# Weight halves split one by one in the attention, kept in memory and reloaded slot by slot

## The chip, the cores and the metric

The kernel runs on one core of a Trainium2 chip. The metric is the device time of one launch in microseconds, as the median of several runs of the kernel. Profiles come from one execution each.

## The reference

Two layers work on 2048 latent tokens and 256 context tokens, 1024 wide, in float32. Layer 0 mixes a gated short convolution with a state-space scan in both directions. Layer 1 is latent attention: 16 heads, queries and keys of 64 + 32 elements (the 32 rotated), values of 64, every latent token attending to all 2304 tokens, then

```python
out_l = (att_l.reshape(b_, n, MLA_MIX) * jax.nn.silu(g_l)) @ w_out   # 2048 x 1024 @ 1024 x 1024
h = h + (gate[:, None] * out_l)
```

where the gate g_l is a 2048 x 1024 product of the normalized input with a 1024 x 1024 part of the layer's input weight, and gate is a vector of the modulation. The change concerns the two 1024 x 1024 weights of these products (the gate's and w_out) while the attention runs.

## The kernel before, in words

A float32 product is made of three float32r matmuls (mm3, lines 119 to 121): each operand is split into a high half (rounded to float32r) and a low half (the rest); high x high, high x low and low x high are summed in PSUM.

The attention is the last stage. It is software-pipelined by hand: one loop over steps t (from line 2129 on), 64 items (a head and a block of 512 queries) of 9 steps each, 576 steps, and a short tail. A step takes 256 of the 2304 keys. In step t the loop writes out, in this order, the scores of step t (6 matmuls, `scores`), the product of probabilities and values of step t - 16 (18 matmuls, `pv`, L2011), the copy of the scores from PSUM (ScalarE, L1929) and their running maximum (VectorE, L1941) of step t - 1, the conversion to f16 of t - 14 (ScalarE L1985, every third on GpSimd L1983), the exponential of t - 13 (ScalarE, L1975), the subtraction of the maximum of t - 12 (VectorE, L1970) and the low f16 half of t - 15 (GpSimd, L1991). The order that is written is the order on each engine's queue. The score PSUM has two buffers. All DMAs are issued on SyncE's queue (SP), which works them off in the order written.

Beside this run the side products, a generator `side` that is called three times in each step from step 7 on (`side_step`). One product (one mm3 of 512 columns) takes three calls, that is one step. There are six sets: the gate's columns 0 to 511 and 512 to 1023 (16 jobs of 8 products each, `gate_job`), and four sets of the output product (`out_job`): tokens of the first or second half of the blocks, with k 0 to 3 or 4 to 7 of the 8 slices of 128 head columns (in the last set only 4 and 5; 6 and 7 follow in `tail`). A set uses 8 weight slots of 128 x 512, each as high and low half (`wfs(0, s)`, `wfs(1, s)`), held in SBUF tiles named t, v and u. The left operand of a job comes by DMA into a tile named at (1 MB for a gate job, 512 KB or 256 KB for an output job), fetched one job ahead.

`products` runs one set. It first splits the set's 8 slots, one in three calls, so one per step; no product is issued in that time. For a gate slot ScalarE makes the high half (L1728) and GpSimd the low half (L1734). For an output slot, whose weight is scaled, GpSimd first multiplies by the modulation gate (L1740), ScalarE scales and rounds (L1730), VectorE makes the low half (L1736). The raw weights come by DMA into four tiles named raw, four ahead. The first set's slots 0 to 3 were split before the attention. Both halves of the output weight are split twice, for the first and for the second half of the tokens. Before a job whose tile was not fetched ahead, `products` waits two steps (`idle(2)`); an output job also waits until `turner` has gated, transposed and stored the heads that it needs. `turner` starts on a group of heads at the step `ready` of its last head; for the third output set that is step 442 of the schedule's count, and its first tile is stored some steps later.

`later(n, phase, fn)` writes out fn n steps on, at a named place in the step. `f_room` lets a new accumulation start only if one of the two PSUM tiles named fps is free.

Of the kernel before, what the change touches and what calls it, by code (L numbers as in the profile page):

```python
# [10 lines left out]
F32 = mybir.dt.float32  # L11
F32R = mybir.dt.float32r
# [45 lines left out]
def hybrid_conv_s5_mla_kernel(tc, x, c, ctx, c_ctx, mod_w, mod_b, norm_w, e_w_in, e_conv_w, e_lam_re, e_lam_im,  # L58
# [11 lines left out]
    with ExitStack() as top:  # L70
# [3 lines left out]
        def dt(name, shape, dtype=F32):  # L74
            return dr.tile(shape, dtype, name=name)
# [18 lines left out]
        gd = dt("gd", [16, P, D])  # L94
        ad = dt("ad", [16, P, D])
        atd = dt("atd", [16, P, 2, KD, P])

        def plain(a):
            return a.bitcast(F32) if a.dtype == F32R else a
# [1552 lines left out]
        with ExitStack() as at_:  # L1652
# [43 lines left out]
            def wfs(a, s):  # L1696
                return wf_tile(a, s)
# [22 lines left out]

            raw = []

            def w_split():
                w, s, n, scaled = raw.pop(0)

                def hi():
                    if scaled is None:
                        S.copy(out=wfs(0, s), in_=w)  # L1728
                    else:
                        S.activation(out=wfs(0, s), in_=w, func=AF.Copy, scale=invc[:, scaled:scaled + 1])  # L1730

                def lo():
                    if scaled is None:
                        GP.tensor_tensor(out=wfs(1, s), in0=w, in1=wfs(0, s).bitcast(F32), op=ALU.subtract)  # L1734
                    else:
                        V.scalar_tensor_tensor(out=wfs(1, s), in0=w, scalar=invc[:, scaled:scaled + 1],  # L1736
                                               in1=wfs(0, s).bitcast(F32), op0=ALU.mult, op1=ALU.subtract)

                if scaled is not None:
                    GP.tensor_tensor(out=w, in0=w, in1=g1[:, n], op=ALU.mult)  # L1740
                later(1, "pre", hi)
                later(1, "post", lo)
# [2 lines left out]
                for _ in range(3 * n):  # L1745
                    yield

            def products(slots, jobs, ahead, first=0):

                for x_ in range(first, len(slots)):  # L1750
                    yield
                    yield
                    w_split()
                    if x_ + 4 < len(slots):
                        w_raw(slots[x_ + 4:x_ + 5])
                    yield
                tiles = {}

                def fetch(m):
                    if m < len(jobs):  # L1760
                        tiles[m] = jobs[m][0]()

                for m, (_, mats, evac, need) in enumerate(jobs):
                    if m not in tiles:
                        while need and need not in turned:
                            yield from idle(1)
                        fetch(m)
                        yield from idle(2)
                    a, rest = tiles.pop(m)
                    for x_, (k, s) in enumerate(mats):  # L1770
                        yield
                        while x_ == 0 and not f_room():
                            yield
                        if x_ == 0:
                            ps = f_get()
                        mm3(ps, a[:, 0, k, :], a[:, 1, k, :], wfs(0, s), wfs(1, s), x_ == 0, x_ == len(mats) - 1)
                        yield
                        if m + 1 < len(jobs) and m + 1 not in tiles and not unstored and (
                                not jobs[m + 1][3] or jobs[m + 1][3] in turned):
                            fetch(m + 1)  # L1780
                        if x_ == len(mats) - 1:
                            evac(ps, rest)
                            if m == len(jobs) - 2:
                                w_raw(ahead[:4])
                        yield

            def gate_job(lt, n):
# [18 lines left out]
            def out_job(lt, n, k0, k1):  # L1806
                ns = slice(n * 512, (n + 1) * 512)
                j, b = lt // 2, lt % 2

                def load():  # L1810
                    a = big.tile([P, 2, KD, P], F32R, name="at", bufs=2)
                    ht = (wt.tile([P, 512], F32, name="raw", bufs=4) if k1 == 6 else wk.tile([P, 512], F32, name="fo"))
                    dma(out=a[:, :, k0:k1], in_=atd[lt, :, :, k0:k1])
                    dma(out=ht, in_=hd[lt, :, ns])
                    return a, ht

                def evac(ps, ht):
                    def add():
                        V.tensor_tensor(out=ht, in0=ps, in1=ht, op=ALU.add)
                        f_put()  # L1820

                    def store():
                        dma(out=(ol[b, :, j, ns] if k1 == KD else hd[lt, :, ns]), in_=ht)
                        unstored.discard((lt, n))

                    if k1 != 6:
                        unstored.add((lt, n))
                    later(1, "mid", add)
                    later(1, "post", store)

                return load, [(k, k % 4 + 4 * n) for k in range(k0, k1)], evac, (lt, k0)
# [5 lines left out]
            def turner():  # L1837

                for l0_, l1_, k0, k1, every in ((0, 8, 0, 4, 12), (0, 8, 4, 8, 6), (8, 16, 0, 4, 7), (8, 16, 4, 6, 4),
                                                (8, 12, 6, 7, 3), (12, 16, 6, 7, 3)):  # L1840
                    kn = k1 - k0
                    cs = slice(k0 * P, k1 * P)
                    for lt in range(l0_, l1_):
                        while now[0] < max(ready[lt // 4, k] for k in range(k0, k1)) or (now[0] + 5) % NP < 2:
                            yield
                        a = wk.tile([P, 512], F32, name="ta", bufs=3)
                        gt = wk.tile([P, 512], F32, name="tg", bufs=2)
                        dma(out=a[:, :kn * P], in_=ad[lt, :, cs])
                        dma(out=gt[:, :kn * P], in_=gd[lt, :, cs])

                        def gated(a=a, gt=gt, kn=kn):
                            GP.tensor_tensor(out=a[:, :kn * P], in0=a[:, :kn * P], in1=gt[:, :kn * P], op=ALU.mult)

                        later(3, "post", gated)

                        def turn(a=a, lt=lt, k0=k0, kn=kn):
                            ps = f_get()
                            for k in range(kn):
                                PE.transpose(ps[:, k * P:(k + 1) * P], a[:, k * P:(k + 1) * P], idf)
                            m = wk.tile([P, 2, 4, P], F32R, name="tm", bufs=1)  # L1860
                            pv = ps[:, :kn * P].rearrange("p (k n) -> p k n", k=kn)

                            def store():
                                dma(out=atd[lt, :, :, k0:k0 + kn], in_=m[:, :, :kn])
                                turned.add((lt, k0))

                            def low():
                                V.tensor_tensor(out=m[:, 1, :kn], in0=pv, in1=m[:, 0, :kn].bitcast(F32), op=ALU.subtract)
                                f_put()

                            later(1, "pre", lambda: S.copy(out=m[:, 0, :kn], in_=pv))
                            later(1, "mid", low)
                            later(1, "post", store)

                        later(5, "turn", turn)
                        turns_due.add(now[0] + 5)
                        for _ in range(every):
                            yield
# [11 lines left out]
                return [out_job(lt, n, k0, k1) for lt in range(l0_, l1_) for n in range(2)]  # L1890

            def side():
                yield from products(gslots(0), [gate_job(lt, 0) for lt in range(16)], gslots(1), first=4)
                yield from products(gslots(1), [gate_job(lt, 1) for lt in range(16)], kslots(0))
                yield from products(kslots(0), out_jobs(0, 8, 0, 4), kslots(4))
                yield from products(kslots(4), out_jobs(0, 8, 4, 8), kslots(0))
                yield from products(kslots(0), out_jobs(8, 16, 0, 4), kslots(4))
                yield from products(kslots(4), out_jobs(8, 16, 4, 6), [])


            vt_ = {}
# [204 lines left out]
            tails = [tail(2, total, total + 4, 0), tail(3, total + DP + 1, total + DP + 2, total + 8)]  # L2106
            sd = side()
            alive = [True]

            tn = turner()  # L2110

            def side_step():
                if alive[0] and next(sd, "end") == "end":
                    alive[0] = False

# [6 lines left out]
            while t < total + DP + 2 or alive[0] or agenda or tails:  # L2122
# [14 lines left out]
                if t > 6:  # L2137
                    side_step()
                next(tn, None)
                if t < total:  # L2140
                    g, h, qb = its[i]
                    if p == 0 and i + 1 < NI:
# [88 lines left out]
```

## Time and profile before

| what | us |
|---|---|
| median of 3 runs (3537.05 to 3541.81) | 3540.95 |
| the profiled execution | 3544.93 |
| its span | 3542.9 |
| TensorE busy in the span | 3241.8 |
| VectorE busy | 2633.4 |
| ScalarE busy | 2187.5 |
| GpSimd busy | 2153.3 |

The span runs from the first to the last instruction of the profiled execution. Matmuls are pipelined, and one begins before the one ahead of it has ended, so the distance of their starts is what one costs. An instruction's duration on VectorE can hold time in which it stands still. The granted clock of TensorE is given as a share of full speed; 1.00 is 2.4 GHz, 0.50 is 1.2 GHz. Copies of the scores (L1929) are counted to know how many steps a stretch holds.

### The profile page before, as it was taken

What the parts mean: (1) busy time and instruction counts of PE and PEld (TensorE: products, weight loads), DVE (VectorE), ACT (ScalarE), POOL (GpSimd) and SP (SyncE); (2) the same over time, 40 slices, a digit from 0 to 9 for tenths busy, and PEclk for the clock granted to TensorE, in tenths of its full rate; (3) what the DMA queues carried; (4) which work ended last, traced back from release to release, by engine and by line L of the source; (5) the groups of instructions that cost most, each with busy time, mean ns of one, the idle gap of its engine ahead of it and who ended that gap; (6) DMA issues with size and microseconds to landing.
All of it is one profiled execution on the core that took longest, in us unless ns stands there. A gap on an engine that the chain in (4) does not pass through costs nothing. (4 is left out here: it accounts for less than half of the span.)

```text
span 3542.9 us, 63798 instructions
## 1 busy us (share of the span) xinstructions
PE 3241.8 (92%) x24725; PEld 2702.8 (76%) x24725; DVE 2633.4 (74%) x3974; ACT 2187.5 (62%) x2889; POOL 2153.3 (61%) x1347
## 2 busy tenths in 40 slices
PE   5988999989889888888799998999989999899897
PEld 4877877777767778888588887888868788688786
DVE  5766328483367676666688887888898988989897
ACT  4211322221333354444599999999989899899895
POOL 2455022222465323233388889888888988899996
PEclk9998999999999999999899999999999999899998
DMA  7333856654576656776843444445356555366584
GB/s 198 118 103 103 269 143 166 185 157 136 167 245 225 200 122 158 161 164 147 217 120 105 129 125 132 147 135 152 105 154 200 169 140 158 101 188 184 158 251 140
DMA packets 487517, 564.89 MB, mean 159 GB/s; under 512 B 83443, under 2 KB 353224, under 8 KB 479152
## 3 DMA queue, kind: packets, MB, share of 16 engines
q1 hardware_dynamic: 476080, 543.97, 54.6%
q0 software_dynamic: 2688, 8.46, 0.7%
q10 hardware_dynamic: 8448, 8.39, 0.7%
q8 instruction: 196, 3.21, 0.4%
q14 instruction: 105, 0.86, 0.1%
HBM read 378.17 MB, written 182.54 MB: 158 GB/s over the span
## 5 line engine op out<-in xcount | busy, mean ns | idle before, releaser
L1991 POOL TENSOR_TENSOR pl<-S,ph 128x1024 f16<-128x1024 f32 x430 | 918.0, 2159 | 14.5 <-ACT ph L1985 13.8
L1970 DVE TENSOR_TENSOR S<-S,t 128x1024 f32<-128x1024 f32 x432 | 520.6, 1211 | 36.9 <-PE t L1965 35.7
L1941 DVE TENSOR_TENSOR rm<-s,rm 128x1024 f32<-128x1024 f32 x384 | 468.5, 1220 | 81.0 <-ACT S L1929 62.5
L1975 ACT ACTIVATE S<-S,psh 128x1024 f32<-128x1024 f32 x432 | 498.6, 1154 | 48.1 <-DVE S L1970 47.9
L319 PE MATMUL accps<-aT,wh 128*128 128x480 f32 (+2 forms) x1920 | 491.2, 386 | 8.1 <-ACT wh L113 6.3
L119 PE MATMUL s<-q,K 96*128 96x512 f32 x1134 | 462.2, 408 | 39.4 <-DVE rm L1941 29.2
L1929 ACT COPY S<-s 128x1024 f32<-128x1024 f32 x432 | 435.5, 1008 | 58.1 <-PE s L121 53.8
L120 PE MATMUL s<-q,K 96*128 96x512 f32 x1134 | 452.3, 399 | 0.0
L121 PE MATMUL s<-q,K 96*128 96x512 f32 x1134 | 451.2, 398 | 0.0
L2011 PE MATMUL O<-Vy,ph 128*128 128x129 f16 (+2 forms) x5760 | 441.3, 211 | 0.0
L319 PEld LDWEIGHTS accps<-aT,wh 128*128 128x128 f32 x1920 | 343.2, 193 | 73.0 <-issue 18.0
L2011 PE MATMUL O<-Vy,pl 128*128 128x65 f16 x4608 | 338.2, 196 | 39.0 <-POOL pl L1991 27.4
L2011 PEld LDWEIGHTS <-pl 128*128 128x128 f16 x4608 | 242.9, 99 | 162.0 <-issue 84.2
L1985 ACT CAST ph<-S 128x1024 f16<-128x1024 f32 x288 | 302.4, 1050 | 18.7 <-PE O L2011 14.2
L1991 POOL TENSOR_TENSOR pl<-Sy,ph 128x1024 f16<-128x1024 f32 x142 | 305.3, 2170 | 7.9 <-DVE ph L1981 4.1
L2011 PEld LDWEIGHTS <-ph 128*128 128x128 f16 x5760 | 289.5, 99 | 0.0
L119 PEld LDWEIGHTS s<-q,K 96*128 96x128 f32 x1134 | 216.8, 191 | 94.6 <-DVE rm L1941 19.7
L319 PE MATMUL accps<-aT,wl 128*128 128x480 f32 (+2 forms) x960 | 265.5, 374 | 8.5 <-POOL wl L116 8.5
L121 PEld LDWEIGHTS s<-q,K 96*128 96x128 f32 x1134 | 216.7, 191 | 48.9
L120 PEld LDWEIGHTS s<-q,K 96*128 96x128 f32 x1134 | 218.1, 192 | 46.0
L116 POOL TENSOR_TENSOR wl<-w,wh 128x1024 fp32r<-128x1024 f32 x25 | 61.6, 2465 | 256.7 <-ACT wh L113 237.9
L319 PEld LDWEIGHTS accps<-aT,wl 128*128 128x128 f32 x960 | 175.4, 192 | 37.6 <-POOL wl L116 9.8
(509 smaller groups left out, 7314.6 us busy)
## 6 DMA issues: line engine op xcount, KB each, us to landing
at<-a1d SPq DMA_DIRECT2D x47, 1024.0 KB
K<-kd SPq DMA_DIRECT2D x101, 384.0 KB
w<-in_e_w_in_dram SPq DMA_DIRECT2D x48, 512.0 KB
at<-atd SPq DMA_DIRECT2D x48, 512.0 KB
Vy<-vd SPq DMA_DIRECT2D x34, 580.5 KB
K<-krd SPq DMA_DIRECT2D x101, 192.0 KB
mw<-in_mod_w_dram SPq DMA_DIRECT2D x64, 256.0 KB
a1d<-at SPq DMA_DIRECT2D x16, 1024.0 KB
```

The lines of the kernel that those rows point to most:

```text
L116: el.tensor_tensor(out=lo, in0=src, in1=hi.bitcast(F32), op=ALU.subtract)
L119: PE.matmul(ps, lh, rh, start=start, stop=False)
L120: PE.matmul(ps, lh, rl, start=False, stop=False)
L121: PE.matmul(ps, ll, rh, start=False, stop=stop)
L319: PE.matmul(a_[:, 0:(j1 - j0) * q], lw[:, k, :], rt[:, k, j0 * q:j1 * q], start=(k == 0 and lw is wh and rt is aT[0]), stop=(k == KD - 1 a ...
L1929: S.copy(out=st["S", p], in_=st["ps", p])
L1941: V.tensor_tensor(out=rm, in0=ps, in1=st["S", 0] if p == 1 else rm, op=ALU.max)
L1970: V.tensor_tensor(out=sb, in0=sb, in1=state[i]["mb"][:, None, :].to_broadcast([P, 2, 512]), op=ALU.subtract)
L1975: S.activation(out=sb, in_=sb, func=AF.Exp, scale=scale, bias=psh[:, 0:1])
L1985: S.copy(out=st["ph", p], in_=st["S", p])
L1991: e.tensor_tensor(out=st["pl", p], in0=st["S", p], in1=st["ph", p], op=ALU.subtract)
L2011: PE.matmul(part(r_, v.shape[-1]), w[:, a, r_ * P:(r_ + 1) * P], v, start=(c_ == 0 and n == 0), stop=(c_ == 17 and n == 8), skip_group_che ...
```

## The change

The splitting moves out of `products`. A new generator `prep`, called once a step from step 14 on, loads one raw slot, splits it into the tile wh (high half) and, in place, raw (low half), and stores both in device memory (`wsd`, 3 sets of 8 slots), one slot in 11 steps: the gate's second set, then the output weight's k 0 to 3 and 4 to 7. Each is split once. Only the first set's slots 4 to 7 are still split in `products`, ahead of its first job. `products` now runs all six sets as one list of jobs. After the last use of a slot in a set, its two halves are reloaded from `wsd` for the next set, one step later. Until step 441 every eighth call of `side_step` does nothing, which spreads the products. The residual's tile of every output job is now taken from the raw tiles, and ta has two buffers in place of three.

```diff
+        wsd = dt("wsd", [3, 8, 2, P, 512])
...
-            def w_split():
-                w, s, n, scaled = raw.pop(0)
-
+            def w_split(w, n, scaled, wh, wl):
                 def hi():
                     if scaled is None:
-                        S.copy(out=wfs(0, s), in_=w)
+                        S.copy(out=wh, in_=w)
                     else:
-                        S.activation(out=wfs(0, s), in_=w, func=AF.Copy, scale=invc[:, scaled:scaled + 1])
+                        S.activation(out=wh, in_=w, func=AF.Copy, scale=invc[:, scaled:scaled + 1])
 
                 def lo():
                     if scaled is None:
-                        GP.tensor_tensor(out=wfs(1, s), in0=w, in1=wfs(0, s).bitcast(F32), op=ALU.subtract)
+                        GP.tensor_tensor(out=wl, in0=w, in1=wh.bitcast(F32), op=ALU.subtract)
                     else:
-                        V.scalar_tensor_tensor(out=wfs(1, s), in0=w, scalar=invc[:, scaled:scaled + 1],
-                                               in1=wfs(0, s).bitcast(F32), op0=ALU.mult, op1=ALU.subtract)
+                        V.scalar_tensor_tensor(out=wl, in0=w, scalar=invc[:, scaled:scaled + 1], in1=wh.bitcast(F32),
+                                               op0=ALU.mult, op1=ALU.subtract)
...
-            def products(slots, jobs, ahead, first=0):
-
-                for x_ in range(first, len(slots)):
-                    yield
-                    yield
-                    w_split()
-                    if x_ + 4 < len(slots):
-                        w_raw(slots[x_ + 4:x_ + 5])
+            def prep(sets, every):
+
+                for x_, slots in enumerate(sets):
+                    for s, src, n, scaled in slots:
+                        w = wt.tile([P, 512], F32, name="raw", bufs=4)
+                        dma(out=w, in_=src)
+                        for _ in range(3):
+                            yield
+                        wh = wt.tile([P, 512], F32R, name="wh")
+                        w_split(w, n, scaled, wh, w.bitcast(F32R))
+
+                        def store(x_=x_, s=s, wh=wh, w=w):
+                            dma(out=wsd[x_, s, 0], in_=wh)
+                            dma(out=wsd[x_, s, 1], in_=w)
+
+                        later(2, "post", store)
+                        for _ in range(every - 3):
+                            yield
+
+            def products(sets):
+
+                for _, s, n, scaled in list(raw):
+                    yield
+                    yield
+                    w_split(raw.pop(0)[0], n, scaled, wfs(0, s), wfs(1, s))
                     yield
                 tiles = {}
+                jobs = []
+                after = {}
+                for x_, (_, js) in enumerate(sets):
+                    last = {}
+                    for m, j in enumerate(js):
+                        for y, (_, s) in enumerate(j[1]):
+                            last[s] = (len(jobs) + m, y)
+                    if x_ + 1 < len(sets):
+                        for s in range(8):
+                            after.setdefault(last.get(s, (len(jobs), 0)), []).append((sets[x_ + 1][0], s))
+                    jobs += js
+
+                def reload(todo):
+                    for x_, s in todo:
+                        for a in range(2):
+                            dma(out=wfs(a, s), in_=wsd[x_, s, a])
...
                         mm3(ps, a[:, 0, k, :], a[:, 1, k, :], wfs(0, s), wfs(1, s), x_ == 0, x_ == len(mats) - 1)
+                        if (m, x_) in after:
+                            later(1, "post", lambda todo=after[m, x_]: reload(todo))
...
-                            if m == len(jobs) - 2:
-                                w_raw(ahead[:4])
...
-                    ht = (wt.tile([P, 512], F32, name="raw", bufs=4) if k1 == 6 else wk.tile([P, 512], F32, name="fo"))
+                    ht = wt.tile([P, 512], F32, name="raw", bufs=4)
...
-                        a = wk.tile([P, 512], F32, name="ta", bufs=3)
+                        a = wk.tile([P, 512], F32, name="ta", bufs=2)
...
-                yield from products(gslots(0), [gate_job(lt, 0) for lt in range(16)], gslots(1), first=4)
-                yield from products(gslots(1), [gate_job(lt, 1) for lt in range(16)], kslots(0))
-                yield from products(kslots(0), out_jobs(0, 8, 0, 4), kslots(4))
-                yield from products(kslots(4), out_jobs(0, 8, 4, 8), kslots(0))
-                yield from products(kslots(0), out_jobs(8, 16, 0, 4), kslots(4))
-                yield from products(kslots(4), out_jobs(8, 16, 4, 6), [])
+                yield from products([
+                    (None, [gate_job(lt, 0) for lt in range(16)]), (0, [gate_job(lt, 1) for lt in range(16)]),
+                    (1, out_jobs(0, 8, 0, 4)), (2, out_jobs(0, 8, 4, 8)),
+                    (1, out_jobs(8, 16, 0, 4)), (2, out_jobs(8, 16, 4, 6))])
...
+            calls = [0]
+            SIDE = ready[2, 3]
...
+            pr = prep([gslots(1), kslots(0), kslots(4)], 11)
+
             def side_step():
+
+                calls[0] += 1
+                if now[0] < SIDE and calls[0] % 8 == 0:
+                    return
                 if alive[0] and next(sd, "end") == "end":
                     alive[0] = False
...
+                if t > 13:
+                    next(pr, None)
```

## Rows read from the trace of the kernel before

**Rows 1.** The page's first part: busy us, share of the span, instructions of each engine.
```profile
PE 3241.8 (92%) x24725; PEld 2702.8 (76%) x24725; DVE 2633.4 (74%) x3974; ACT 2187.5 (62%) x2889; POOL 2153.3 (61%) x1347
```
**Rows 2.** Windows: length; PE, PEld, DVE, ACT, POOL busy (count); clock; DMA share; GB/s.
```profile
1767.20:2134.30 367.10, 366.79 (x3461) 298.76 (x3458) 315.30 (x332) 337.50 (x347) 311.13 (x179) 1.00 0.40 118
...
3117.40:3303.00 185.60, 185.60 (x1763) 152.52 (x1761) 167.93 (x183) 170.60 (x175) 164.70 (x98) 1.00 0.67 192
3356.50:3452.10 95.60, 95.60 (x927) 79.22 (x926) 91.27 (x107) 89.59 (x96) 85.36 (x56) 1.00 0.88 249
...
3452.10:3480.00 27.90, 24.66 (x254) 19.55 (x250) 26.14 (x31) 26.94 (x32) 26.67 (x19) 1.00 0.42 120
```
**Rows 3.** Windows of ScalarE's L1929 alone: length, busy (count); granted clock, DMA share, GB/s.
```profile
1767.20:3480.00 1712.80, 563.68 (x559) 0.98 0.51 149
2134.30:2175.30 41.00, 12.19 (x13) 0.92 0.39 129
2556.30:2609.10 52.80, 12.99 (x13) 0.84 0.39 108
2794.40:2840.50 46.10, 12.91 (x13) 0.93 0.37 111
3021.70:3110.40 88.70, 26.03 (x26) 0.88 0.38 104
3303.00:3350.70 47.70, 12.01 (x12) 0.86 0.41 117
3452.10:3480.00 27.90, 10.13 (x10) 1.00 0.42 120
```
**Rows 4.** Windows of TensorE's matmuls on the tiles named at, same columns.
```profile
1767.20:3480.00 1712.80, 447.80 (x1428) 0.98 0.51 149
2134.30:2175.30 41.00, 1.89 (x6) 0.92 0.39 129
...
3303.00:3350.70 47.70, 2.57 (x6) 0.86 0.41 117
```
**Rows 5.** Timeline of TensorE in two steps: start us, us, instruction.
```profile
1915.29 0.48 PE L119 MATMUL fps<-v,at 128*128 128x512 f32 x1
...
1918.16 0.48 PE L119 MATMUL fps<-u,at 128*128 128x512 f32 x1
...
2560.00 0.47 PE L119 MATMUL s<-q,K 96*128 96x512 f32 x1
...
2562.17 0.48 PE L119 MATMUL s<-q,K 96*128 96x512 f32 x1
```
**Rows 6.** Instructions on the tile raw: duration ns min/median/max, first and last start us.
```profile
L102 SPq DMA_DIRECT2D raw<-in_o_w_out_dram x32: 327/338/1525, 2527.9 to 3326.7; - x32
L1740 POOL TENSOR_TENSOR raw<-raw,g x32: 1262/1294/1800, 2560.2 to 3337.8; 128x512 f32<-128x512 f32 x32
...
L1736 DVE SCALAR_TENSOR_TENSOR t<-raw,invc,t x16: 737/1458/8854, 2566.2 to 3325.3; 128x512 fp32r<-128x512 f32 x16
...
L1734 POOL TENSOR_TENSOR t<-raw,t x4: 1286/1287/1289, 2145.1 to 2156.1; 128x512 fp32r<-128x512 f32 x4
```
**Rows 7.** Timeline of VectorE, POOL and TensorE around two scaled low halves.
```profile
3051.05 2.14 POOL L1991 TENSOR_TENSOR pl<-S,ph 128x1024 f16<-128x1024 f32 x1
...
3052.14 1.60 DVE L1736 SCALAR_TENSOR_TENSOR v<-raw,invc,v 128x512 fp32r<-128x512 f32 x1
...
2566.20 8.85 DVE L1736 SCALAR_TENSOR_TENSOR t<-raw,invc,t 128x512 fp32r<-128x512 f32 x1
...
2566.87 1.28 POOL L1740 TENSOR_TENSOR raw<-raw,g 128x512 f32<-128x512 f32 x1
...
2572.38 2.13 POOL L1991 TENSOR_TENSOR pl<-Sy,ph 128x1024 f16<-128x1024 f32 x1
...
2576.34 0.77 PE L119 MATMUL s<-q,K 96*128 96x512 f32 x1 [8.47 <-DVE rm L1941]
```
**Rows 8.** What SP's queue waited for, 1767 to 3480 us: total, times, longest.
```profile
SPq L102 <- PE s L121: 329.8, 92, 21.0
```

## The prediction

> **What bounds the kernel now.** I read the page's first part, then the stretches of the attention stage, then the matmuls of single steps, then the split's own instructions. TensorE is busy for 92% of the span [rows 1], but that is an average. The attention runs 576 steps; the copy that empties the score PSUM (L1929) runs once in each, so its count in a stretch is a count of steps. From 1767.2 to 3480.0 us there are 559 steps in 1712.8 us [rows 3]. Inside the stretches in which the side products run, TensorE has no gap: 366.79 of 367.10 us, 185.60 of 185.60, 95.60 of 95.60, with the clock granted in full (1.00, the 2.4 GHz level), while VectorE, ScalarE and GpSimd are at 85 to 95% [rows 2]. There the matmuls are the bound.
>
> Between them lie five stretches in which the products pause, because the next eight weight slots are split then: one split a step, then two steps for the first tile, and in the fourth also the wait for gated heads. They hold 13, 13, 13, 26 and 12 steps in 41.0, 52.8, 46.1, 88.7 and 47.7 us [rows 3]: 77 steps in 276.3 us, 3.59 each, though only 13 products fall into them (39 matmuls on the tiles named at; the first and the last of the five stand in [rows 4]). A step with less matmul work is longer there than a step with all of it. The granted clock falls to 0.84 to 0.93 as a mean of these stretches, so part of each is at the 1.2 GHz level, after TensorE had stood idle [rows 3].
>
> The remaining 559 - 77 - 10 = 472 steps take 1712.8 - 276.3 - 27.9 = 1408.6 us, 2.984 each. The ten steps at the end without products take 27.9 us, 2.79 each, with ScalarE at 26.94 and POOL at 26.67 us busy [rows 2, 3]: that is about what the other three engines need when the products don't set the pace.
>
> **The change part by part.**
>
> *Products without pauses.* A step with a product runs from 1915.29 to 1918.16 us, 2.87; one without, in a pause that had not yet stalled, from 2560.00 to 2562.17, 2.17 [rows 5]. A product is thus 0.70 us of TensorE. Of 476 products (1428 matmuls, [rows 4]) 13 lie in the pauses and one in the last ten steps, so 462 in the 472 steps: a step without one costs 2.984 - 0.70 x 462/472 = 2.30 on average, transposes included. If only TensorE counted, the 77 pause steps would cost 77 x 2.30 + 13 x 0.70 = 186 us in place of 276: **90 us less**, wherever the products are put. That is the floor, and it holds while products are spread so that TensorE always has work.
>
> Are they? Up to step 441 one call in eight of the side work is skipped, so seven products come in eight steps. Counted by calls (4 splits, 256 gate products, 128 output products, 3 calls each), both gate sets end near step 307 and the first two output sets near 455; then the heads needed by the third (due at step 447) are there, and the last ends near 559, as before. Only the tail without products grows, by some 5 steps: 5 x (2.79 - 2.30) = **+2.5 us**.
>
> *The skipped steps.* In 435 steps about 55 have no product. TensorE needs 2.30 there, but the other engines 2.79. If nothing evens this out, that is 55 x 0.49 = 27 us; if the two score buffers let TensorE run ahead and stay ahead, 0. The product steps show TensorE without a gap beside engines that are 85 to 95% busy [rows 2], so I lean to the low end: **+8**.
>
> *Splits.* 44 in all become 4 + 24 = 28: each half-size piece (k 0 to 3 and 4 to 5) is no longer split twice. The 24 move into steps 14 to 278, one in eleven, beside products. A scaled one costs POOL 1.29 us and VectorE 1.46 in the median of the 16 on t, an unscaled one POOL 1.29 [rows 6], each with one copy on ScalarE. Back to back they cost, above 2.79 a step: (52.8 - 36.3)/8 = 2.1, (46.1 - 36.3)/8 = 1.2 and (47.7 - 33.5)/8 = 1.8 each in the second, third and fifth pause, and (41.0 - 36.3)/8 = 0.6 in the first, unscaled. That is the upper end: 16 x 2.1 + 8 x 0.6 = 38 us. The lower end is 0: ten free steps follow each one, and VectorE and POOL have 0.3 to 0.4 us to spare per step [rows 2]. A delayed pl or rm still reaches TensorE, which has no reserve now, so I take about half of the pauses' mean: 16 x 0.9 + 8 x 0.3 = **+17**.
>
> The scaled low half on VectorE is where the price is uncertain. It stands still while POOL works: one started at 3052.14, when POOL's pl of 3051.05 had 1.05 us to go, and took 1.60; another started at 2566.20, took 8.85 us and ended half a us after POOL's pl of 2572.38, the last of five POOL instructions that had followed without a gap; TensorE then stood for 8.47 us [rows 7]. The Trainium skill ("SBUF — State Buffer", Who interferes with whom) has it that a VectorE instruction with two SBUF inputs and a GpSimd instruction that reads SBUF exclude each other, and that the one which came first keeps the port for its whole length. The first of these rows agrees. By that rule no low half would wait for more than one POOL instruction, 16 x 2.2 = 35 us of VectorE at most; the second row differs, since five were let past.
>
> *Reloads and stores.* 80 reloads and 48 stores of 256 KB are added and 16 loads go: 112 more issues on SP, about 0.34 us each as for raw [rows 6], 38 us in all. SP waits 329.8 us for score matmuls alone [rows 8], which hides them. A store waits for the split's low half, with K, q and at loads behind it in SP's order; it is issued two steps after, and those loads come eight or more steps ahead of use: nothing. If that cover goes, one late q is a step, 3 us. A reload waits for the product that read the slot last, one step earlier; the slot is needed again eight products later, some 20 us after the issue.
>
> The bytes matter more. One set is 4.2 MB within eight steps, 24 us. The transfers move 192 GB/s at a share of 0.67, so some 287 at full share (an estimate from that row); 4.2 MB are 15 us of all engines beside 0.67 x 24 = 16 that are there already [rows 2]. So up to 7 us of backlog at each of five borders, less in the gate stretch (share 0.40). Bounds 0 and 35; eight steps' lead should cover most: **+6**. The Trainium skill ("DMA: Bandwidth & Descriptors", Specifications) puts the fabric's ceiling at 435 GB/s; an estimate by that page has 10 us for a set, no backlog, and this term at 0. The trace doesn't come near that: 249 GB/s go with a share of 0.88 [rows 2].
>
> *No cost*: ta with two buffers in place of three (its pieces are freed after 5 steps and asked for every 3 at the closest, two apart), and the residual's tile in the raw buffers, which prep has left by step 278, before the first output job.
>
> Sum: 90 - 2.5 - 8 - 17 - 6 = 56 us. The profiled execution took 3544.9 us, 2 above its span of 3542.9; it lies 4 us (0.1%) above the median of 3540.95. So 3544.9 - 56 = 3489 for its like, 3485 against the median.
>
> **The rivals.**
>
> *The floor* (0.12): splits, skips and bytes all hide. 3541 - 88 = 3453. For it: ten free steps per split. Against: no engine has more than 15% to spare.
>
> *The other engines take over* (0.20): skipped steps cost 27, splits 38 as in the pauses, bytes 6: 90 - 2.5 - 71 = 17 left, 3524. For it: ScalarE and POOL at 96% in the steps without products [rows 2]. Against: those steps come singly now.
>
> *The low halves starve* (0.05), the slower end: each of the 16 is let in only when POOL runs dry, as at 2566.20. POOL's split instruction comes one step ahead and fills just that gap. 16 x 8.5 = 136 us in place of 14: 3485 + 122 = 3607. It decides from some seven of the 16 on. Against: the median of the 16 on t is 1.46 [rows 6]; a VectorE that stands soon dries POOL out.
>
> *Reloads come late* (0.04): transfers keep to SP's order, and a backlog of one step at the first product of each reloaded slot, 40 x 2 us, takes back 80: 3565. Against: 20 us of lead.
>
> **How the numbers follow.** The forecast, 3485, has 0.59, with its own range 3462 to 3510. Below 0.2% (7 us) a measurement of this kernel can't tell a change. Faster holds with the forecast, the floor and nearly all of the third case: 0.89; the same 0.02, from that case's end; slower 0.09, the two last. The range, 3450 to 3525, takes in the floor and the third case; what is left out is the slower pair and some at either end.
>
> **What would show it.** The changed profile should have one step per 2.9 us from about 1767 to 3425 without the five stretches of 3.6, the granted clock at 1.00 throughout, 16 scaled low halves (32 before) at 1.5 to 2.2 us, and products in seven of eight steps. Wrong would be: low halves of 8 us with TensorE waiting for rm behind them (starving); TensorE waiting for DMA at the set borders near steps 159, 307, 383, 455 and 523 (bytes); or no waits of that kind and yet steps above 2.95, with ScalarE or POOL near 100% (others take over).

## The result

The changed kernel took 3494.43 us in the median (3490.34 to 3503.67, 4 runs) against 3539.84 for the kernel before: a ratio of 0.9876, 95% interval 0.9853 to 0.9899. Run again beside later experiments it took 3504.49 us (3492.90 to 3518.03, 6 runs) against 3535.41, 0.9915 (0.9896 to 0.9933). The gain is 31 to 45 us; 56 were forecast, 3485 us, in a range of 3450 to 3525. The changed kernel spreads more from run to run (25 us over those six) than the versions without VectorE's low half (e4 7 us, e12 5, e7 12); a likely reason follows below.

From the page of the changed kernel: busy time by engine, and the granted clock in 40 slices of the span.

```profile
PE 3222.4 (92%) x24725; PEld 2685.1 (77%) x24725; DVE 2605.1 (75%) x3958; ACT 2174.0 (62%) x2873; POOL 2130.2 (61%) x1331
...
PEclk9998999999999899999899999999999999999998
```

TensorE's share is still 92% [rows 1]: the share is blind to this change. Two sets of windows tell more. First the copies of the scores (L1959 now), which count steps; columns as in [rows 3]. The first stretch holds the 559 steps that were 1712.8 us; the second, steps 280 to 292, is where the second pause was; the third, from step 518 to 530, holds the last reloads.

```profile
1759.70:3425.80 1666.10, 562.68 (x560) 1.00 0.58 171
...
2557.10:2592.10 35.00, 11.96 (x13) 1.00 0.43 137
...
3259.00:3296.70 37.70, 12.12 (x13) 1.00 0.89 275
```

The same 559 steps take 46.7 us less. Where 13 steps had taken 52.8 us at a clock of 0.84, twelve take 35.0 at 1.00, with ten products in them. Then all engines, columns as in [rows 2]: all 559 steps, the steps 100 to 278 with the scaled splits, the steps 278 to 441 with skipped calls alone, and the end without products.

```profile
1759.70:3425.80 1666.10, 1629.56 (x15459) 1319.73 (x15456) 1483.31 (x1580) 1532.25 (x1588) 1472.94 (x871) 1.00 0.58 171
2005.50:2551.20 545.70, 525.15 (x4933) 421.33 (x4932) 486.74 (x498) 495.07 (x519) 480.50 (x282) 0.99 0.51 154
2551.20:3028.30 477.10, 473.11 (x4512) 384.23 (x4509) 423.34 (x458) 440.76 (x449) 418.67 (x244) 1.00 0.59 171
3379.30:3425.80 46.50, 42.42 (x432) 33.59 (x430) 43.54 (x51) 45.23 (x53) 44.15 (x32) 1.00 0.47 130
```

TensorE has gaps of 1666.10 - 1629.56 = 36.5 us left. Of these 20.5 lie in the 178 steps of the second line (3.07 us each), 4.0 in the 163 steps of the third (2.93 each). What stands there is in the split's instructions, columns as in [rows 6]:

```profile
L1739 POOL TENSOR_TENSOR raw<-raw,g x16: 1281/1289/1345, 2018.0 to 2526.5; 128x512 f32<-128x512 f32 x16
...
L1735 DVE SCALAR_TENSOR_TENSOR raw<-raw,invc,wh x16: 745/1905/7306, 2025.0 to 2531.4; 128x512 fp32r<-128x512 f32 x16
```

One of the 16 scaled low halves took 7.31 us. The timeline around it (start, us), as in [rows 7]:

```profile
2225.00 7.31 DVE L1735 SCALAR_TENSOR_TENSOR raw<-raw,invc,wh 128x512 fp32r<-128x512 f32 x1
...
2225.45 6.31 POOL L2021 TENSOR_TENSOR pl<-Sy,ph 128x1024 f16<-128x1024 f32 x3
...
2233.49 0.79 PE L120 MATMUL s<-q,K 96*128 96x512 f32 x1 [4.96 <-DVE rm L1971]
```

(pl is the low f16 half of the probabilities, made on GpSimd; rm the running maximum, made on VectorE.) The low half ended half a microsecond after GpSimd's third pl in a row, and TensorE stood for 4.96 us for the maximum queued behind it.

### The profile page after: what moved, and what is told of

Same layout as the page of the kernel before. It is cut to its first block, busy times and chain, and to the rows that moved or that the text cites. A ratio compares the mean times of both kernels' runs of the same rounds, so it can differ in the third digit from the quotient of the medians.

```text
span 3489.0 us, 63902 instructions
## 1 busy us (share of the span) xinstructions
PE 3222.4 (92%) x24725; PEld 2685.1 (77%) x24725; DVE 2605.1 (75%) x3958; ACT 2174.0 (62%) x2873; POOL 2130.2 (61%) x1331
## 4 chain that ended last, share of the span: by engine, by line
PE 56%; DVE 14%; POOL 13%; issue 6%; DMA 5%; ACT 4%; SPq 1%; POOLq 0%; ACTq 0%; DVEq 0%
PE accps L320 11%; POOL pl L2021 8%; PE O L2041 7%; PE s L120 5%; PE s L121 5%; PE s L122 5%; PE fps L120 2%; PE fps L122 2%; PE fps L121 2%; PE s5ps L967 2%; POOL ph L2013 2%; PE accA L121 2%; PE accA L122 2%; PE accA L120 2%; PE accB L122 1%
## 5 line engine op out<-in xcount | busy, mean ns | idle before, releaser
L1959 ACT COPY S<-s 128x1024 f32<-128x1024 f32 x432 | 434.5, 1006 | 41.7 <-PE s L122 29.3
L120 PEld LDWEIGHTS s<-q,K 96*128 96x128 f32 x1134 | 213.8, 189 | 71.8 <-DVE rm L1971 15.6
L122 PEld LDWEIGHTS s<-q,K 96*128 96x128 f32 x1134 | 213.2, 188 | 47.9
L121 PEld LDWEIGHTS s<-q,K 96*128 96x128 f32 x1134 | 215.0, 190 | 40.4
```

Of the source, the lines that this page charges most:

```text
L120: PE.matmul(ps, lh, rh, start=start, stop=False)
L121: PE.matmul(ps, lh, rl, start=False, stop=False)
L122: PE.matmul(ps, ll, rh, start=False, stop=stop)
L1959: S.copy(out=st["S", p], in_=st["ps", p])
```

## The experiments

Times are medians in us, ratios are to the kernel before. It was run anew beside e1 to e4 (3534.51), e5 to e8 (3537.48) and e9 to e12 (3535.41), so ratios compare across these three groups.

**e1, no splits in prep.**

```diff
-                        wh = wt.tile([P, 512], F32R, name="wh")
-                        w_split(w, n, scaled, wh, w.bitcast(F32R))
...
-                            dma(out=wsd[x_, s, 0], in_=wh)
+                            dma(out=wsd[x_, s, 0], in_=w)
```

> Changed kernel, but the 24 prepared slots are not split: the raw weight is loaded and stored twice, so all DMAs stay and the multiplies, copies and low halves of these slots are left out (the side products of the later sets are then not the reference's). Theory A (what is left of the pauses' cost sits in the spread splits, above all in the scaled ones of steps 100 to 278, 3.07 us a step against 2.93 later): about 25 us below the changed kernel, near 3469, and the steps 100 to 278 at 2.93. Theory B (it sits in skipped calls, reloads and stores, which are all kept): within 7 us of the changed kernel, 3487 to 3501.

Measured 3471.04, ratio 0.9818 (0.9802 to 0.9833). The steps 100 to 278 and all 559 steps, all engines:

```profile
2010.90:2535.40 524.50, 517.85 (x4931) 420.22 (x4930) 453.92 (x482) 487.28 (x502) 455.10 (x266) 1.00 0.53 160
1766.40:3409.60 1643.20, 1621.63 (x15463) 1318.72 (x15460) 1450.30 (x1564) 1520.10 (x1564) 1437.64 (x847) 1.00 0.59 173
```

The first line is 21.2 us less than with the splits: TensorE's gaps there fall from 20.5 to 6.7 us, and its busy time by 7.3. Theory A: by the ratios the spread splits cost 20 to 34 us in the whole, though every one has ten free steps behind it.

**e2, no skipped calls.**

```diff
-                if now[0] < SIDE and calls[0] % 8 == 0:
+                if now[0] < 0 and calls[0] % 8 == 0:
```

> Changed kernel without the skipped calls: one product in each step until the fourth set is done near step 398, then some 53 steps without a product until the heads for the fifth set are there. Theory A (TensorE is the bound, and a step without a product falls from 2.98 only to some 2.75 in a row, but to 2.30 when single): some 15 us above the changed kernel, near 3510. Theory B (the skip itself wastes TensorE's time in the first 441 steps): at or below the changed kernel, 3480 to 3494.

Measured 3512.77, 0.9938 (0.9922 to 0.9954). The size is near A's, the reason isn't. Windows of the steps 100 to 278, 278 to 441 and 441 to 558:

```profile
2006.30:2568.70 562.40, 542.08 (x5002) 437.94 (x5001) 498.18 (x502) 497.70 (x521) 478.93 (x282) 0.98 0.55 165
2568.70:3043.70 475.00, 462.75 (x4462) 374.14 (x4458) 423.52 (x457) 438.15 (x445) 417.95 (x244) 1.00 0.57 168
3043.70:3403.30 359.60, 343.86 (x3243) 281.55 (x3242) 314.31 (x348) 317.16 (x331) 309.20 (x187) 0.98 0.69 199
```

Against the first profile of the changed kernel that is +16.7, -2.1 and +8.6 (its last stretch, 3028.3 to 3379.3 us, takes 351.0). So most of the loss in this profile lies in the split's stretch, where three low halves took 7.3, 7.9 and 6.1 us; the gathered wait of 53 steps costs about 6.5. That leaving out the skips makes more low halves long is not shown: the executions with them had one, two and three long ones (the first profile; e11; e8 and e9), those without three and four (e2, e3).

**e3, the pauses put back without the splits** (as e2, and ten idle steps at each set).

```diff
+                    first.add(len(jobs))
...
+                    if m and m in first:
+                        yield from idle(10)
```

> Changed kernel without the skipped calls, and with ten steps without products put back at each set's start: the pauses of the kernel before, at their places, but with no split in them (prep still splits beside the products). Theory A (both the missing products and the splits made the pauses dear): pause steps near 2.75 in place of 3.59, the whole near 3517, half way between the two kernels. Theory B (a pause without splits costs nothing, all was the splits): 3495 or less. Theory C (the pause alone is the cost, splits hid in it): 3535 or more.

Measured 3506.72, 0.9920 (0.9905 to 0.9934). Here the twelve steps 280 to 292 and the thirteen 353 to 366 (columns as in [rows 3]):

```profile
2585.50:2617.80 32.30, 11.96 (x12) 1.00 0.47 129
2803.20:2838.50 35.30, 12.98 (x14) 1.00 0.59 155
```

2.7 us a step without a split in it, where the kernel before needed 49.8 (2559.3 to 2609.1 us) and 46.1 us for the same steps. The whole of the steps 278 to 441, with the matmuls of the side products counted (columns as in [rows 4]), the kernel before and then e3:

```profile
2553.40:3077.40 524.00, 122.59 (x390) 0.96 0.52 151
```
```profile
2579.60:3057.20 477.60, 122.55 (x390) 1.00 0.60 174
```

The same 130 products (390 matmuls) with the pauses at the same places; what has gone is the splits, and reloads stand for the loads of raw weights. That is 46.4 us. So what made these pauses dear was the split in each step. The changed kernel, which spreads its products, takes 477.1 us there as well, with 140 products in them. A pause alone loses what a step without a product can't give back: 2.7 instead of 2.3.

The whole of e3, 3507, lies between A's 3517 and B's 3495. The splits that left the pauses stand in the steps 100 to 278 and are paid there: 566.0 us (2013.6 to 2579.6) against 538.2 in the kernel before (2015.2 to 2553.4), both with 167 products. Four of e3's 16 low halves took 5.0 to 8.1 us.

**e4 and e12, the scaled low half on GpSimd.** ScalarE scales in place.

```diff
-                        S.activation(out=wh, in_=w, func=AF.Copy, scale=invc[:, scaled:scaled + 1])
+                        S.activation(out=w, in_=w, func=AF.Copy, scale=invc[:, scaled:scaled + 1])
+                        S.copy(out=wh, in_=w)
...
-                        V.scalar_tensor_tensor(out=wl, in0=w, scalar=invc[:, scaled:scaled + 1], in1=wh.bitcast(F32),
-                                               op0=ALU.mult, op1=ALU.subtract)
+                        GP.tensor_tensor(out=wl, in0=w, in1=wh.bitcast(F32), op=ALU.subtract)
```

> Changed kernel, the scaled low half moved off VectorE: ScalarE scales the raw tile in place and copies it rounded (0.7 us more), GpSimd subtracts (1.3 us more), VectorE does nothing for a split. Theory A (the scaled split's price is VectorE standing while GpSimd holds the way): TensorE's gaps in steps 100 to 278 fall from 20 us to under 10, the whole about 8 to 12 us below the changed kernel, near 3484. Theory B (the price is GpSimd's own load, which grows by 20 us here): 5 to 20 us above it, 3500 to 3515.

Measured 3480.14, 0.9843 (0.9828 to 0.9858). Once more as e12, beside the changed kernel itself (e11):

> e4 once more, beside the changed kernel. Theory A (the low half is better kept off VectorE): 8 to 14 us below the changed kernel of this call. Theory B (e4's difference was the chip's): within 4 us of it.

> The changed kernel itself, beside the next one on the same chip. Both theories: 3485 to 3500; a spread of 10 us from run to run, since one to three low halves starve in some runs and not in others.

e12 3482.92, 0.9849 (0.9837 to 0.9862); e11 3504.49. Steps 100 to 278, e12 and then e11:

```profile
2006.30:2539.00 532.70, 520.53 (x4931) 419.70 (x4929) 454.66 (x482) 503.38 (x534) 494.65 (x298) 1.00 0.52 157
```
```profile
2009.40:2559.90 550.50, 526.47 (x4933) 422.66 (x4932) 490.21 (x498) 495.16 (x519) 479.81 (x282) 0.99 0.51 152
```

GpSimd works 15 us more and ScalarE 8, VectorE 36 less; TensorE's gaps are halved, 12.2 for 24.0 (A wanted under 10). Theory A holds, and the gain is 22 us beside e11, more than it said; against the first measurement it is 12 by the ratios. e11 itself came out above the 3485 to 3500 expected. Its profile has two long low halves (7.31 and 6.27 us) where the first profile of the same code had one, and that execution took 11 us longer (3502.02 against 3490.75). Two profiles don't show that the spread of the changed kernel comes from this, but it fits. e4 is the fastest version of the study that computes everything, 1.5 to 1.6% below the kernel before.

**e5 and e6, the place of the split in the item's nine steps.** One slot in 9 steps, begun at step 20 or 15.

```diff
-            pr = prep([gslots(1), kslots(0), kslots(4)], 11)
+            pr = prep([gslots(1), kslots(0), kslots(4)], 9)
...
-                if t > 13:
+                if t > 19:
```

e6 has `t > 14` in the last line.

> Changed kernel, prepared slots one in 9 steps in place of 11, begun at step 20: each raw slot is then loaded in the third step of an item. In the traces of e2 and e3, where the split runs through all nine places, the scaled low half took 0.74 us at this one. Theory A (what a scaled split costs is how long VectorE is shut out by GpSimd, and the place in the item's nine steps decides that): all 16 near 0.75 us, no gap of TensorE behind them, 10 to 18 us below the changed kernel, near 3478. Theory B (each split has one price, wherever it stands): 3488 to 3500.

> The same with the start at step 15, so that each raw slot is loaded in the seventh step of an item, where the scaled low half took 7.5 and 6.1 us in e3. Theory A (place decides): most of the 16 at 5 to 8 us, TensorE standing 3 to 5 us behind each, 50 to 80 us above the changed kernel, 3540 to 3575, that is no faster than the kernel before. Theory B (one price for all places): 3488 to 3500, as e5.

e5 3494.45, 0.9878 (0.9859 to 0.9897); e6 3579.09, 1.0125 (1.0107 to 1.0143), **slower than the kernel before**. The low halves of e5, then of e6 with one example:

```profile
L1735 DVE SCALAR_TENSOR_TENSOR raw<-raw,invc,wh x16: 742/746/1564, 1999.8 to 2414.6; 128x512 fp32r<-128x512 f32 x16
```
```profile
L1735 DVE SCALAR_TENSOR_TENSOR raw<-raw,invc,wh x16: 1526/6272/7502, 1978.2 to 2479.2; 128x512 fp32r<-128x512 f32 x16
...
2110.53 6.26 DVE L1735 SCALAR_TENSOR_TENSOR raw<-raw,invc,wh 128x512 fp32r<-128x512 f32 x1
...
2109.92 6.33 POOL L2021 TENSOR_TENSOR pl<-S,ph 128x1024 f16<-128x1024 f32 x3
2123.26 1.04 POOL L2013 CAST ph<-S 128x1024 f16<-128x1024 f32 x1 [7.01 <-PE O L2041]
...
2009.40:2637.50 628.10, 557.53 (x4930) 448.96 (x4929) 545.06 (x497) 497.05 (x517) 473.42 (x281) 0.93 0.44 132
```

The place decides nearly all of how long VectorE is shut out: the low half takes 0.75 us in the median at one, 6.27 at the other, where it meets three pl in a row. The two kernels differ in one number, and in 85 us. In e6 the 178 steps take 628.1 us; 15 of the 16 low halves start in them, so each split costs (628.1 - 524.5)/15 = 6.9 us against e1.

The GpSimd line behind the three pl tells more than their number. After the third, GpSimd has nothing to do for 7 us: the low half was let in only when GpSimd had run dry. It is so for all 33 low halves of more than 5 us in the nine profiles that have them on VectorE (the kernel before, the changed one twice, e2, e3, e5, e6, e8, e9): GpSimd's next instruction starts 2.8 us or more after the low half's end. Most of the others that met GpSimd got in between two of its instructions, as this one of the changed kernel did; the pl that followed takes 2.60 us where pl alone takes about 2.15:

```profile
2192.62 1.73 DVE L1735 SCALAR_TENSOR_TENSOR raw<-raw,invc,wh 128x512 fp32r<-128x512 f32 x1
```
```profile
2193.76 2.60 POOL L2021 TENSOR_TENSOR pl<-S,ph 128x1024 f16<-128x1024 f32 x1
```

But e5's second half of A failed: 3478 was forecast, and with VectorE free e5 has the ratio of the changed kernel's first measurement, 13 us under that of the second, so no clear gain. TensorE's gaps in steps 100 to 278 are 541.4 - 521.9 = 19.5 us, and now wait on others (engine, line waited for: us, times, longest; O is the product of probabilities and values, A an item's finished output):

```profile
PE O L2041 <- POOL pl L2021: 5.3, 13, 0.5
PE O L2041 <- DVE A L2055: 4.2, 7, 1.2
PE O L2041 <- issue: 3.3, 2, 2.3
```

**e7, e4's split at e5's place.**

> Low halves on GpSimd as in e4, and the place of e5. Theory A (with VectorE out of the split the place matters little, only GpSimd's own 2.6 us a split is left): 3473 to 3484, within 5 us of e4's 3480. Theory B (GpSimd's load has a good place too, the one where it would wait for the probabilities): 3465 to 3473.

Measured 3498.21, 0.9885 (0.9868 to 0.9902): neither. e4, which runs through all nine places, is better by 13 to 15 us. The place that suits VectorE is a bad one for the end of an item: in the steps 100 to 278 TensorE waits 4.6 us for A in e7 and 0.8 in e12, here in this order:

```profile
PE O L2041 <- DVE A L2055: 4.6, 7, 1.3
```
```profile
PE O L2041 <- DVE A L2055: 0.8, 2, 0.6
```

That is part of the 11 us by which these steps take longer in e7 (543.5 against 532.7). Which of the split's instructions delays A was not varied.

**e8, every half reloaded twice; e9, the same bytes copied within device memory instead.**

```diff
-                        for a in range(2):
+                        for a in (0, 1, 0, 1):
                             dma(out=wfs(a, s), in_=wsd[x_, s, a])
```

That is e8; e9 has this instead:

```diff
+        wsx = dt("wsx", [3, 8, 2, P, 512])
...
                             dma(out=wfs(a, s), in_=wsd[x_, s, a])
+                            dma(out=wsx[x_, s, a], in_=wsd[x_, s, a])
```

> Changed kernel, each half reloaded twice, one after the other: 8.4 MB per set in place of 4.2, 80 more DMAs on the queue. Theory A (eight steps of lead hide the reloads; the changed kernel's trace has 3 us of TensorE waiting for a DMA): 2 to 12 us above the changed kernel, 3496 to 3506. Theory B (the bytes at the set borders cost, as the prediction's rival had it): 20 us or more above, with TensorE waiting for DMAs at the borders near steps 159, 307, 383, 455 and 523.

> Changed kernel; beside each reloaded half, the same 256 KB are copied once more from device memory to device memory, to a place that nothing reads. The bytes of e8's second reload, but no transfer has to wait on SP for another one to land. Theory A (e8 lost its 122 us because each second reload waited on SP's queue until the first had landed, with the left operands and score inputs behind it): at most 25 us above the changed kernel, below 3520. Theory B (e8's loss was the bytes at the set borders): 60 us or more above, 3555 and up.

e8 3616.15, 1.0227 (1.0211 to 1.0243); e9 3528.08, 0.9975 (0.9963 to 0.9987), 24 above the changed kernel measured beside it. What SP's queue waited for in e8 (total, times, longest), then TensorE:

```profile
SPq L103 <- DMA t<-wsd: 81.1, 39, 7.0
...
SPq L103 <- DMA v<-wsd: 40.0, 20, 5.9
SPq L103 <- DMA u<-wsd: 37.3, 20, 5.0
```
```profile
PE fps L120 <- DMA at<-atd: 65.0, 6, 18.3
```

A second load into the same place waits on the queue until the first has landed; 79 such waits, 158 us in all, hold up the left operands behind them. So e8 has the size of B but not its cause. e9 has no such wait and loses 24 us, as its A says, in place of the 110 to 124 of e8 (by the ratios against the two measurements of the changed kernel); it misses A's 3520 because the changed kernel beside it was slow as well. Of the 24, 18 stand in the steps 453 to 530 (253.7 against 235.7 us in e11), at the last two borders. At the later one TensorE waits for the left operand (first line); for the 7.2 us at the earlier one, ahead of the same kind of matmul, the profile names nothing that it waited for (second line):

```profile
PE fps L121 <- DMA at<-atd: 11.5, 2, 9.1
PE fps L121 <- issue: 7.2, 2, 5.9
```

The steps 278 to 441, with two borders, take 477.2 us in both. The rest of e9's loss in the trace lies in steps 100 to 278, where a third low half was long (8.49 us), so the bytes themselves cost some 18 in this trace.

**e10, e4 without the skipped calls.**

> Low halves on GpSimd as in e4, without the skipped calls as in e2. Theory A (three of the 16 low halves starved in e2 because a product in every step leaves GpSimd's queue without a gap; the gathered wait of 53 steps itself cost only 6 us there): 5 to 12 us above e4, 3485 to 3492, with no stretch of more than 5 us without a matmul in steps 100 to 278. Theory B (the gathered wait is what the skip avoids): as far above e4 as e2 lies above the changed kernel, 18 to 24 us, 3498 to 3504.

Measured 3489.69, 0.9873 (0.9859 to 0.9888), 7 above e12: Theory A. With the low halves off VectorE the skip is worth 7 us; with them on it 8 to 22, by e2's ratio against the two of the changed kernel.

## Why the prediction was right, point by point

- **The floor, 90 us less.** Right: TensorE's own work was to be 1712.8 - 90 = 1623 us wherever the products stand. Without the splits (e1) it is busy for 1621.63 us of these steps, in the changed kernel for 1629.56; the 8 us between them come with the splits. The heading that the 90 us stand under, products without pauses, is less right: e3 keeps the pauses, without splits in them, and has 46 us of the gain in the steps 278 to 441. All of an old pause above 2.7 us a step was the split, the rest the missing product.
- **Skipped steps, +8.** Right in size: 4.0 us of gaps in the 163 steps that have nothing else, so about 11 in 435. That TensorE runs ahead over a single step without a product fits this; e10 has the gathered form at 7 us more. The growth of the tail, +2.5, didn't come: 46.5 us for the 17 steps from 558, 47.5 before (3432.5 to 3480.0).
- **Splits, +17.** Too low, and more than half of what the 559 steps took above the sum (1712.8 - 56 = 1657; measured 1666.1, and 1675.3 in e11, 1763.0 to 3438.3 us). e1 prices them at 21.2 + 1.3 (steps 16 to 100, 245.8 against 244.5) = 22.5 us in the first profile, and at 27.8 by the same stretches of e11, where one more low half was shut out (550.5 and 246.3). I took half of what they cost back to back because ten free steps follow. But TensorE is the bound there, and the steps 100 to 278 took 3.07 us each against 2.95 in e1: the free steps gave too little back.
- **Starving, given 0.05.** It is real, not a rival of the whole but a part of it: one or two of the 16 in the changed kernel, up to four in versions with the same spacing (e3), and 15 of 16 in e6, which is the slower case as it was described (3607 forecast; e6 measured 3579). Its condition, let in only when GpSimd runs dry, is what every long low half shows. The place in the item's nine steps decides most of it, but not all: the last low half of the changed kernel took 2.07 us in the first profile and 6.27 in e11, at the same step. The Trainium skill ("SBUF — State Buffer", Who interferes with whom) has it that the one which came first gets the shared ports for its whole instruction. By that a waiting low half would stand behind one GpSimd instruction. In e6's example it stood behind three pl, two of which began after it.
- **Reloads and bytes, +6.** Somewhat high: the changed kernel's TensorE waited 2.8 us for the operands named at, 2.1 of them at the last border, where the transfers reach a share of 0.89 at 275 GB/s. The estimate of nearly full transfers at the borders was borne out by e9: no room for the same bytes once more at the last two borders, room at the two in steps 278 to 441. The terms put at nothing (ta, the raw tiles) no run varied; among the waits of TensorE that the profile lists in the 559 steps neither stands.
- **What the sum couldn't see.** Of the 54 us between the two profiled spans 7.5 lie before the first of the 559 steps (1767.2 against 1759.7 us). That point moves from 1752.0 to 1767.8 over the experiments, in code that they share, so I don't count it to the change. That the profiled execution came within 2 us of the 3489 forecast for its like (3490.75) is luck: without those 7.5 us it would have taken about 3498.

What stays open: why a low half is let in between two GpSimd instructions at some places, and at others only when GpSimd has run dry. In the traces GpSimd's instructions follow one another without a gap in both kinds.

## What to carry to other kernels

When one engine is full in every ordinary step, look for the stretches in which steps with less work of it take longer: what is interleaved there, not what is missing, is the cost, and moving it beside the full steps pays only as far as it disturbs nobody. An instruction of VectorE that must wait for GpSimd belongs off VectorE when something that the bound waits for is queued behind it; here that gained 12 to 22 us. Reloading a buffer one step after its last reader cost TensorE 2.8 us here; what cost over 100 was to have transfers wait on the common queue for others to land.

## What the runs showed of the hardware that was not expected

A VectorE instruction that takes 0.74 us alone took 5.7 to 7.5 us, 15 times in 16, while GpSimd ran three instructions of 2.1 us back to back (e6), and its record counts that time as busy. It was let in when GpSimd had nothing left to run. After such a stand TensorE's granted clock drops as well. Around the long low half of the changed kernel, behind which TensorE stood for 4.96 us until 2233.49:

```profile
2224.00:2232.00 8.00, 4.53 (x53) 3.67 (x50) 7.61 (x2) 5.29 (x6) 7.75 (x5) 1.00 0.16 47
2232.00:2240.00 8.00, 6.51 (x34) 5.38 (x35) 5.71 (x7) 2.32 (x3) 0.22 (x1) 0.57 0.54 160
```

The mean falls from 1.00 to 0.57, so most of the second stretch is at the 1.2 GHz level. Over e6's 178 steps the mean is 0.93, against 1.00 in e1 and e12.
